# A two-layer hybrid trunk on one core: attention weights turned by transfers, heads joined on VectorE, squares read from SBUF, one lo stream tied behind both norms

## The chip, the cores and the metric

One core of one Trainium2 chip runs the whole program. The metric is the device time of one execution in microseconds, and the time of a kernel is the median of its runs. All matmuls, copies and transfers below are on this core's engines: TensorE (PE), VectorE (DVE), ScalarE (ACT), GpSimd (POOL) and the queue of SyncE (SP) that issues most of the transfers.

## The reference

A decoder trunk of two layers on 256 tokens of width 1024, in fp32. Each layer applies three sublayers, each followed by a LayerNorm of a residual:

```python
x <- LN(alpha*x + 0.5*SwiGLU_1(x))
x <- LN(alpha*x + Mixer(x))
x <- LN(alpha*x + 0.5*SwiGLU_2(x))
```

The mixer projects x to u, v, q, k, val and two gates. One branch is a gated position mixing of u and v. The other, which matters here, is differential attention: 8 heads, two softmax maps of head dimension 64 per head, and values of width 128.

```python
q, k = rope(q), rope(k)
p = softmax(where(causal, q @ k.T * scale, neg))       # two maps per head
a = p[:, :, 0] - lam * p[:, :, 1]
o = a @ val                                            # 128 wide per head
h_b = rmsnorm(o) * g * (1 - lam_init)
merge = sigmoid(gate_A)*(h_A W_A) + sigmoid(gate_B)*(h_B W_B)
```

## The kernel before, in words

**Products.** Every fp32 weight tile is split into a hi part (ACT copies it to fp32r, L174) and a lo part (DVE subtracts, L178, `wlo<-raw,whi`). A product then is hi x hi, lo x hi and hi x lo. `gemm_a2` does it for a 256-wide output: per half tile 8 matmuls of 512 columns against x's hi and lo side by side (L283), then, for the lo weights, 8 of 256 columns (L290). ACT copies one half of the bank to `r` (L291), DVE adds the other to give `z` (L293, or L295 with a scale). Pools are small: 4 raw tiles, 8 hi and 8 lo half tiles, 4 main PSUM banks and 4 side banks, each used in turn. A lo half tile is free again when the L290 that read its former content is done; a hi half tile when its L283 is.

**Order.** PE's instructions run as the program writes them (a manual schedule). A clock counts beats of PE work, some 2.8 us each; `beside(task, d)` lets a generator continue d beats later, and its `yield n` puts the rest off by n beats, so that work of other stages falls between the matmuls of a gemm. The other engines are ordered by a scheduler with priorities; `behind(ins)` ties an instruction behind another one on its engine.

**The attention part of the mixer.** After the values, four head pairs run. For each, `rope` makes q and then k: a `gemm_a2` of one tile, four small transfers on SP that swap the rotary halves (L809), POOL's multiplication of `swap` by the sines (L813), DVE's by the cosines (L812) and, tied behind the latest `z`, the addition `qk<-qk,swap` (L817). `attend` of a pair then runs beside the next pair's gemms:

- scores (L837), into two side banks for the second block of queries, and 0.6 beats later into two for the first; DVE masks and takes minima (L845), ACT exponentiates (L847);
- DVE forms the reciprocals and the weighted difference of the two maps (L863, L864, L856);
- 2.6 beats later PE transposes the difference in six 128x128 blocks (L871, L876) into two side banks, and ACT copies these to SBUF (L873, L878);
- 2.3 beats later PE multiplies with the values (L884, L886) into one side bank; ACT copies it to `on` (L889) and squares the bank in place for the sum of squares (L894);
- 2 beats later POOL makes the reciprocal root of four sums (L897, L256 to L264, called `rsqrt4`); 2 beats later ACT scales (L905), splits the 16-bit halves of each word into planes (L184), and one DMA transpose turns them (L189);
- after it has landed, ACT joins the planes (L195), and ACT and DVE write hi and lo of the head outputs (L915, L916).

So a pair takes seven side banks in turn: four for scores, two for transposes, one for the product. Gates follow the four pairs: `gemm_a2` and a tanh on ACT (L932), and their weights are split ahead, while the last pairs' attention still runs.

**The start of an FFN behind a norm.** `gemm_b2` starts with weights split early. The lo parts of its last stream are tied by `after[3]`. A norm's end for token half t is: statistics (L571, L578), a reciprocal root in eight tiny DVE instructions (L241 to L249), two 512-wide normalisations (L582), and PE's transposes of the result (L641). `norm.ends[t]` is the last L582 of half t; `norm.xlo[0, 1]` is a lo split of x that belongs to half 0, so it stands earlier.

Of the kernel before, what the change touches and what calls it, by code (L numbers as in the profile page):

```python
# [13 lines left out]
BF16 = mybir.dt.bfloat16  # L14
I32 = mybir.dt.int32
U16 = mybir.dt.uint16
# [4 lines left out]
P = 128  # L21
D = 1024
T = 256
# [35 lines left out]
def trunk(ctx, tc, x, xT, w13a, w13b, w2s, w2p, wb, wqk, wa, wbr, wo, gateb, sgug, sgub, sguwT, sgubias, lam, diffg,  # L59
# [129 lines left out]
        nc.sync.dma_start_transpose(out=tt.rearrange("p (c t) -> p c t", c=2 * n), in_=pk)  # L189
        return tt  # L190

    def join(dst, tt):

        with behind(emptied[0]):
            A.activation(dst.bitcast(U16).rearrange("p (k w) -> p k w", w=2), tt.rearrange("p (w k) -> p k w", w=2), AF.Copy)  # L195

    def ahead(srcs):

# [178 lines left out]
    def gemm_b2(srcs, xh, xl, done, norm=None):  # L377

        lent, after = [()] * 4, [(None, None)] * 4
        if norm:
            lent = [(0, 1), (0,), (), ()]
            after[1:3] = [(norm.ends[0], norm.ends[0])] * 2
        ps = [[bank() for _ in range(2)] for _ in range(NT)]
        got = [[None] * 4 for _ in range(2)]
        for t in range(NT):
            for c in range(2):
                if norm:
                    norm.ready(t, c)  # L390
                    after[3] = [norm.ends[1] if norm.pre else norm.xlo.get((0, 1))] * 2
                for m in range(2):
                    n = 2 * c + m
                    if t == 0 and n < 2 and norm and norm.pre:
                        if n == 0:
                            got[0][:2], got[1][:2] = rest_of(norm.pre, norm.ends[0])
                    elif t == 0:
                        got[m][2 * c : 2 * c + 2] = stream(srcs[m][:, c * CH : (c + 1) * CH], sub=512, lent=lent[n],
                                                           after=after[n])
                    for i in range(2 * c, 2 * c + 2):  # L400
                        rows_b(ps[t][m], t, 2 * i, got[m][i], xh, xl, KT)
            early[0] = None
            with behind(latest[0] if t == 0 else None):
                done(t, ps[t])
# [383 lines left out]
    def mixer(l, i, norm):  # L788
# [34 lines left out]
        def attend(hp, qT, kT):  # L823
# [38 lines left out]
            first = exps(0)  # L862
            V.reciprocal(out=rc, in_=sums[:, 4:])  # L863
            V.scalar_tensor_tensor(out=c4, in0=rc, scalar=neg_lam[l], in1=sums[:, :4], op0=ALU.mult, op1=ALU.mult)  # L864
            second, first = less(1, second), less(0, first)
            yield 2.6
            b = side_bank()
            for j in range(2):
                for c in range(2):
                    o = (j * 2 + c) * P  # L870
                    PE.transpose(b[:, o : o + P], second[:, o : o + P], ident)  # L871
            aT1 = slots("aT", 2)[0]
            A.activation(aT1, b, AF.Copy)  # L873
            b = side_bank()
            for j in range(2):
                PE.transpose(b[:, j * P : (j + 1) * P], first[:, j * P : (j + 1) * P], ident)  # L876
            aT0 = slots("aT", 2)[0][:, :T]
            A.activation(aT0, b[:, :T], AF.Copy)  # L878
            yield 2.3
            b = side_bank()  # L880
            for j in range(2):
                h = hp * 2 + j
# [5 lines left out]
            on = slots("on", 2)[0]  # L888
            A.activation(on, b, AF.Copy)  # L889
            ss, s2 = sm("ss", 4), sm("s2", 4)  # L890
            A.activation(s2, sums[:, :4], AF.Square, scale=(2 * HD * EPS) ** 0.5)
            for q in range(4):
                s = slice(q * P, (q + 1) * P)
                A.activation(b[:, s], b[:, s], AF.Square, accum_out=ss[:, q : q + 1])  # L894
            yield 2
            with behind(turned_by[0]):
                G.tensor_tensor(out=ss, in0=s2, in1=ss, op=ALU.add)  # L897
# [10 lines left out]
            tt = turning(pk, 4)  # L908
            yield LAND
            b = slots("turned", 2)[0]  # L910
            join(b, tt)
            dl = dgs[:, l : l + 1]
            for j in range(2):
                h, s = hb[hp * 2 + j], slice(j * T, (j + 1) * T)
# [194 lines left out]
```

## Time and the profile before

| | us |
|---|---|
| median of 3 runs | 1217.87 |
| lowest, highest run | 1216.63, 1217.92 |
| profiled execution, its own time | 1218.69 |
| its span in the trace | 1217.0 |
| granted TensorE clock, mean | 0.999 |

The span is what the trace covers; the 1.7 us between it and the execution's own time lie around it. In a timeline a row gives the start and the busy time in microseconds, the engine, the line, the operation, what is written from what, the shape and the count of instructions that the row groups; a bracket gives idle time before it on that engine and what ended it. In the waits, the three numbers are microseconds in total, times and the longest. In the windows, the columns are the window, its length and the busy time of PE, PEld, DVE, ACT and POOL with counts, then the granted clock, the share of the DMA engines and GB/s.

### The profile page before, as it was taken

Reading aid. Unit: us, or ns where it says so; the run is one execution under the profiler, and the core shown is the slowest. Engines: PE = TensorE matmul, PEld = TensorE weight load, DVE = VectorE, ACT = ScalarE, POOL = GpSimd, SP = SyncE. Lnnn points to the kernel's source line nnn. Section 1 sums busy time; section 2 is a strip of 40 time slices with the busy share of each in tenths; the row PEclk is TensorE's granted clock in tenths of the full one; section 3 lists DMA queues with packets and bytes.
Section 4 is the critical chain, followed back from the end, with each engine's and each line's share of the span. In section 5 each row is a group of like instructions: output and inputs, shape, how many; then the busy total and the mean of one; then the engine's idle time right before and its main releaser. Section 6 shows DMA issues by size and latency. Waiting matters only on the chain.

```text
span 1217.0 us, 16530 instructions
## 1 busy us (share of the span) xinstructions
PE 1205.4 (99%) x5961; PEld 1012.6 (83%) x5961; DVE 946.0 (78%) x1540; ACT 852.7 (70%) x1376; POOL 91.4 (8%) x184
## 2 busy tenths in 40 slices
PE   9999999999999999999999999999999999999998
PEld 8888888888888878888888888888888988788886
DVE  6658998875697876589985679988766878757797
ACT  6677677679865576776775776776898555667761
POOL 0100000223300000000000000003341000000000
PEclk9999999999999999999999999999999999999999
DMA  8985566655764748656677665766648456686551
GB/s 319 320 261 174 211 246 219 214 185 171 233 230 143 232 140 300 193 176 216 239 207 271 198 180 208 252 224 198 214 142 274 168 176 213 176 282 206 181 205 48
DMA packets 101346, 257.00 MB, mean 211 GB/s; under 512 B 66528, under 2 KB 67600, under 8 KB 74640
## 3 DMA queue, kind: packets, MB, share of 16 engines
q1 hardware_dynamic: 97296, 243.03, 59.8%
q0 software_dynamic: 3536, 12.13, 3.1%
q8 instruction: 46, 0.75, 0.2%
q10 hardware_dynamic: 432, 0.79, 0.2%
q14 instruction: 36, 0.29, 0.1%
HBM read 235.47 MB, written 1.05 MB: 194 GB/s over the span
## 4 chain that ended last, share of the span: by engine, by line
PE 91%; DVE 5%; ACT 2%; issue 1%; SPq 0%; DMA 0%; POOL 0%; DVEq 0%; ACTq 0%; POOLq 0%
PE bank L271 35%; PE sbank L271 24%; PE bank L283 16%; PE bank L290 8%; PE sbank L283 2%; PE bank L446 2%; PE sbank L290 1%; DVE wlo L178 1%; PE sbank L837 1%; PE sbank L969 1%; ACT pp L847 0%; ACT whi L174 0%; DVE nwa L248 0%; PE sbank L886 0%; DVE x L234 0%
## 5 line engine op out<-in xcount | busy, mean ns | idle before, releaser
L178 DVE TENSOR_TENSOR wlo<-raw,whi 128x1024 fp32r<-128x1024 f32 (+1 forms) x396 | 436.8, 1124 | 143.1 <-ACT whi L174 112.7
L174 ACT ACTIVATE whi<-raw 128x1024 fp32r<-128x1024 f32 (+1 forms) x396 | 372.9, 971 | 126.3 <-PE bank L283 44.9
L271 PE MATMUL bank<-whi,x 128*128 128x512 f32 x840 | 264.4, 391 | 0.0
L271 PEld LDWEIGHTS bank<-whi,x 128*128 128x128 f32 x840 | 158.6, 189 | 33.1
L271 PE MATMUL bank<-wlo,x 128*128 128x512 f32 x420 | 164.2, 391 | 0.0
L271 PE MATMUL sbank<-whi,x 128*128 128x512 f32 x512 | 158.9, 389 | 0.0
L283 PE MATMUL bank<-x,whi 128*128 128x512 f32 x640 | 156.0, 394 | 0.0
L283 PEld LDWEIGHTS bank<-x,whi 128*128 128x128 f32 x640 | 117.1, 188 | 26.4 <-issue 2.3
L271 PEld LDWEIGHTS sbank<-whi,x 128*128 128x128 f32 x512 | 96.1, 188 | 20.0
L353 ACT ACTIVATE shi<-raw 128x1024 fp32r<-128x1024 f32 (+1 forms) x80 | 73.4, 947 | 52.3 <-DVE raw L368 26.4
L271 PE MATMUL sbank<-wlo,x 128*128 128x512 f32 x256 | 99.6, 389 | 0.0
L355 DVE TENSOR_TENSOR slo<-raw,shi 128x1024 fp32r<-128x1024 f32 (+1 forms) x80 | 85.4, 1087 | 14.2 <-ACT shi L353 13.3
L271 PEld LDWEIGHTS bank<-wlo,x 128*128 128x128 f32 x420 | 79.2, 188 | 16.3
L290 PE MATMUL bank<-x,wlo 128*128 128x256 f32 x640 | 85.9, 285 | 0.0
L290 PEld LDWEIGHTS bank<-x,wlo 128*128 128x128 f32 x640 | 81.6, 191 | 2.2
L291 ACT ACTIVATE r<-bank 128x256 f32<-128x256 f32 x112 | 41.8, 377 | 24.5 <-PE bank L290 24.2
L271 PEld LDWEIGHTS sbank<-wlo,x 128*128 128x128 f32 x256 | 48.1, 188 | 9.9
L271 PE MATMUL sbank<-whi,hhi 128*128 128x512 f32 x144 | 56.3, 391 | 0.0
L271 PE MATMUL sbank<-whi,hlo 128*128 128x512 f32 x144 | 56.1, 389 | 0.0
L271 PE MATMUL sbank<-wlo,hhi 128*128 128x512 f32 x144 | 56.0, 389 | 0.0
L506 POOL DMA_DIRECT2D bc<-in_lng x6 | 3.2, 530 | 703.1 <-DVE bc L505 703.1
L710 ACT ACTIVATE planes<-silu 128x1024 uint16<-128x1024 uint16 x40 | 42.0, 1053 | 7.4 <-DVE silu L709 6.2
(249 smaller groups left out, 1996.8 us busy)
## 6 DMA issues: line engine op xcount, KB each, us to landing
raw<-in_w13b SPq DMA_DIRECT2D x76, 1024.0 KB, 5.4
raw<-in_w2p SPq DMA_DIRECT2D x24, 1024.0 KB, 4.9
raw<-in_wa SPq DMA_DIRECT2D x24, 1024.0 KB, 5.2
raw<-in_w2s SPq DMA_DIRECT2D x20, 1024.0 KB, 4.9
raw<-in_wb SPq DMA_DIRECT2D x16, 1024.0 KB, 5.3
raw<-in_wqk SPq DMA_DIRECT2D x16, 1024.0 KB, 4.9
raw<-in_wbr SPq DMA_DIRECT2D x16, 1024.0 KB, 4.8
raw<-in_w13a SPq DMA_DIRECT2D x8, 1024.0 KB, 4.8
```

The costliest lines, as they stand in the source:

```text
L174: copied = A.activation(h, r, AF.Copy)
L178: V.tensor_tensor(out=w, in0=r, in1=h.bitcast(F32), op=ALU.subtract)
L271: PE.matmul(ps, xx, w, start=start and n == 0, stop=stop and n == 2)
L283: PE.matmul(b[-1], hi[:, k * P : (k + 1) * P], xc(k), start=k == 0, stop=False)
L290: PE.matmul(b[n][:, :T], lo[:, k * P : (k + 1) * P], xc(k)[:, :T], start=False, stop=k == KT - 1)
L291: emptied[0] = A.activation(r[:, s], b[n][:, T:], AF.Copy, scale=scale).ins
L353: A.activation(h, r, AF.Copy)
L355: V.tensor_tensor(out=w, in0=r, in1=h.bitcast(F32), op=ALU.subtract)
L446: PE.matmul(ps[t][m], x[:, j, o + t * P : o + (t + 1) * P], y, start=k0 + j == 0 and o == 0 and y is hi, stop=k0 + j == KT - 1 and y is lo)
L710: A.activation(pk.rearrange("p (w k) -> p w k", w=2), s.bitcast(U16).rearrange("p (k w) -> p w k", w=2), AF.Copy)
L837: PE.matmul(banks[m][:, j * nk : (j + 1) * nk], rows(qT, m, j, t * P, P), rows(kT, m, j, 0, nk), start=True, stop=True)
L969: PE.matmul(b[:, j * T + t * P : j * T + (t + 1) * P], vg[t][:, g // 4, s], wsT[g // 4][:, s], start=True, stop=True)
```

## The change

Four edits:

1. The difference of the two maps is no longer transposed by PE. ACT splits it into planes, in a spare `pp` tile that held the other map; SP issues two DMA transposes; 3 beats later DVE joins the planes in two copies (1024 and 512 16-bit elements wide); 3.5 beats after that PE multiplies with the values. The PE transposes, their two side banks and ACT's two copies go. A pair takes five side banks instead of seven.
2. The squares read the SBUF copy `on` and write to a scratch tile, so the bank of the product is read only by the copy to `on`.
3. The join of the head outputs is on DVE, tied behind the latest `z`, instead of ACT.
4. The last lo stream at the start of an FFN is tied behind the norm's end of token half 1 in every case. Before, this held where the weights were split ahead (`norm.pre`), and otherwise (the second FFN of either layer, which follows the mixer) the tie was to `xlo[0, 1]`.

```diff
-    def join(dst, tt):
+    def joined(dst, tt):
 
-        with behind(emptied[0]):
-            A.activation(dst.bitcast(U16).rearrange("p (k w) -> p k w", w=2), tt.rearrange("p (w k) -> p k w", w=2), AF.Copy)
+        with behind(added[0]):
+            V.tensor_copy(dst.bitcast(U16).rearrange("p (k w) -> p k w", w=2), tt.rearrange("p (w k) -> p k w", w=2))
...
-                    after[3] = [norm.ends[1] if norm.pre else norm.xlo.get((0, 1))] * 2
+                    after[3] = [norm.ends[1]] * 2
...
+            free2, free1 = second[1], first[1]
             second, first = less(1, second), less(0, first)
-            yield 2.6
-            b = side_bank()
-            for j in range(2):
-                for c in range(2):
-                    o = (j * 2 + c) * P
-                    PE.transpose(b[:, o : o + P], second[:, o : o + P], ident)
-            aT1 = slots("aT", 2)[0]
-            A.activation(aT1, b, AF.Copy)
-            b = side_bank()
-            for j in range(2):
-                PE.transpose(b[:, j * P : (j + 1) * P], first[:, j * P : (j + 1) * P], ident)
-            aT0 = slots("aT", 2)[0][:, :T]
-            A.activation(aT0, b[:, :T], AF.Copy)
-            yield 2.3
+            half = slots("half", 2)[0]
+            tts = []
+            for (p, spare), dst in (((second, free2), slots("tt", 2)[0]), ((first, free1), half[:, :T])):
+                pk = spare.bitcast(U16)
+                planes(pk, p)
+                tts.append(turning(pk, pk.shape[1] // (2 * P), dst))
+            yield 3
+            aT1, aT0 = slots("aT", 2)[0], half[:, T:]
+            for dst, tt in zip((aT1, aT0), tts):
+                joined(dst, tt)
+            yield 3.5
...
+            junk = s512("junk").bitcast(BF16)
...
-                A.activation(b[:, s], b[:, s], AF.Square, accum_out=ss[:, q : q + 1])
+                A.activation(junk[:, s], on[:, s], AF.Square, accum_out=ss[:, q : q + 1])
...
-            join(b, tt)
+            joined(b, tt)
```

Up to L864 the two kernels have the same line numbers; behind it the new ones are one or two lower for the same code: L889, L905 and L932 of before are L887, L904 and L931 of after.

On DVE, in layer 0, where the scores of the second head pair have been masked and the third pair's `rope` ends (`qk_2336` before and `qk_2333` after are the same rotated k; L856 is the difference of the maps), the rows before are

```order
L845 ISA mx_2315 128x1
L863 RECIPROCAL rc_2318<-sums_2316 128x4
L178 TENSOR_TENSOR wlo_2767<-raw_2764,whi_2766 128x1024
L864 SCALAR_TENSOR_TENSOR c_2317<-rc_2318,neg_lam_818,sums_2316 128x4
L295 SCALAR_TENSOR_TENSOR z_2394<-bank_2353,r_2393 128x256
L856 SCALAR_TENSOR_TENSOR pp_2325<-pp_2330,c_2317,pp_2325 128x256 x2
L856 SCALAR_TENSOR_TENSOR pp_2368<-pp_2373,c_2317,pp_2368 128x128 x2
L817 TENSOR_TENSOR qk_2336<-qk_2336,swap_2335 128x512
L295 SCALAR_TENSOR_TENSOR z_2394<-bank_2384,r_2393 128x256
L178 TENSOR_TENSOR wlo_2771<-raw_2764,whi_2770 128x1024
L812 TENSOR_TENSOR qk_2433<-z_2394,cos_t 128x512
L178 TENSOR_TENSOR wlo_2865<-raw_2862,whi_2864 128x1024
```

and after

```order
L863 RECIPROCAL rc_2315<-sums_2313 128x4
L178 TENSOR_TENSOR wlo_2741<-raw_2734,whi_2740 128x1024
L864 SCALAR_TENSOR_TENSOR c_2314<-rc_2315,neg_lam_818,sums_2313 128x4
L856 SCALAR_TENSOR_TENSOR pp_2322<-pp_2327,c_2314,pp_2322 128x256 x2
L856 SCALAR_TENSOR_TENSOR pp_2365<-pp_2370,c_2314,pp_2365 128x128 x2
L178 TENSOR_TENSOR wlo_2840<-raw_2837,whi_2839 128x1024
L178 TENSOR_TENSOR wlo_2844<-raw_2837,whi_2843 128x1024
L295 SCALAR_TENSOR_TENSOR z_2397<-bank_2350,r_2396 128x256
L817 TENSOR_TENSOR qk_2333<-qk_2333,swap_2332 128x512
L295 SCALAR_TENSOR_TENSOR z_2397<-bank_2387,r_2396 128x256
L812 TENSOR_TENSOR qk_2420<-z_2397,cos_t 128x512
```

Two lo splits and a `z` now stand between L856 and L817, where a `z` ahead of L856 and nothing behind it stood. At the same place one pair earlier there are three splits and a `z` between them now, and nothing before; there the first two splits belong to an earlier tile than the third.

On ACT, in layer 0, around the copy `on` of the second head pair (`on_2636` before, `on_2677` after; `both` is the scaled output of the first pair, `gate` a gate's tanh), the rows before are

```order
L174 ACTIVATE whi_2965<-raw_2959 128x1024
L291 ACTIVATE r_2609<-bank_2568 128x256
L905 ACTIVATE both_2621<-on_2412,nwy_2510 128x128 x4
L184 ACTIVATE both_2621<-both_2621 128x1024
L291 ACTIVATE r_2609<-bank_2599 128x256
L889 ACTIVATE on_2636<-sbank_2629 128x512
L894 ACTIVATE sbank_2629,ss_2638<-sbank_2629 128x128
L174 ACTIVATE whi_3037<-raw_3035 128x1024
```

and after

```order
L184 ACTIVATE pp_2513<-pp_2508 128x1024
L184 ACTIVATE pp_2560<-pp_2555 128x512
L904 ACTIVATE both_2662<-on_2462,nwy_2604 128x128 x4
L174 ACTIVATE whi_3008<-raw_3002 128x1024
L931 ACTIVATE gate_2526<-gz_2611,gbh 128x256 x2
L184 ACTIVATE both_2662<-both_2662 128x1024
L291 ACTIVATE r_2687<-bank_2644 128x256
L291 ACTIVATE r_2687<-bank_2653 128x256
L174 ACTIVATE whi_3081<-raw_3079 128x1024
L887 ACTIVATE on_2677<-sbank_2670 128x512
```

Between the four scalings and `on` there now stand two hi copies and two gate activations as well. `nwy_2604` is POOL's reciprocal root of the first pair; on POOL its instructions stand behind the sine multiplication of the fourth pair's k (`swap_2518`) after the change, and before that multiplication in the kernel before.

On DVE, at the start of the second FFN of layer 0 (`xtok_144` is the residual of token half 1, `yi` to `nwy` its reciprocal root), the rows before are

```order
L244 TENSOR_SCALAR yi_4365<-ve_4364 128x1
L178 TENSOR_TENSOR wlo_4502<-raw_4499,whi_4501 128x512
L248 TENSOR_SCALAR nwa_4368<-yi_4365,ve_4364 128x1
L178 TENSOR_TENSOR wlo_4502<-raw_4499,whi_4501 128x512
L249 TENSOR_SCALAR nwy_4369<-nwa_4368,yi_4365 128x1
L178 TENSOR_TENSOR wlo_4508<-raw_4499,whi_4507 128x512
L248 TENSOR_SCALAR nwa_4372<-nwy_4369,ve_4364 128x1
L178 TENSOR_TENSOR wlo_4508<-raw_4499,whi_4507 128x512
L249 TENSOR_SCALAR nwy_4373<-nwa_4372,nwy_4369 128x1
L248 TENSOR_SCALAR nwa_4376<-nwy_4373,ve_4364 128x1
L249 TENSOR_SCALAR nwy_4377<-nwa_4376,nwy_4373 128x1
L582 TENSOR_SCALAR xtok_144<-xtok_144,mv_4362,nwy_4377 128x512 x2
```

and after

```order
L244 TENSOR_SCALAR yi_4357<-ve_4356 128x1
L248 TENSOR_SCALAR nwa_4360<-yi_4357,ve_4356 128x1
L249 TENSOR_SCALAR nwy_4361<-nwa_4360,yi_4357 128x1
L248 TENSOR_SCALAR nwa_4364<-nwy_4361,ve_4356 128x1
L249 TENSOR_SCALAR nwy_4365<-nwa_4364,nwy_4361 128x1
L248 TENSOR_SCALAR nwa_4368<-nwy_4365,ve_4356 128x1
L249 TENSOR_SCALAR nwy_4369<-nwa_4368,nwy_4365 128x1
L582 TENSOR_SCALAR xtok_144<-xtok_144,mv_4354,nwy_4369 128x512 x2
L178 TENSOR_TENSOR wlo_4494<-raw_4491,whi_4493 128x512 x2
L178 TENSOR_TENSOR wlo_4500<-raw_4491,whi_4499 128x512 x2
```

The four lo splits of the last stream have moved from between the steps of the reciprocal root to behind the normalisation.

## The prediction

> **What bounds the kernel now.** I read the page first: busy time and the chain of work that ended last.
>
> ```profile
> PE 1205.4 (99%) x5961; PEld 1012.6 (83%) x5961; DVE 946.0 (78%) x1540; ACT 852.7 (70%) x1376; POOL 91.4 (8%) x184
> ```
>
> ```profile
> PE 91%; DVE 5%; ACT 2%; issue 1%; SPq 0%; DMA 0%; POOL 0%; DVEq 0%; ACTq 0%; POOLq 0%
> ```
>
> TensorE is busy for 1205.4 of 1217.0 us. The other engines matter only where a matmul waits for them, so the time can change in two ways: PE gets less work, or PE's waits (some 11.6 us in all) change. An engine with 22% idle time can still delay PE if one instruction stands behind the wrong neighbour. The largest wait that this change touches, as total, number and longest:
>
> ```profile
> PE sbank L641 <- DVE xtok L582: 4.7, 2, 2.4
> ```
>
> So I went through PE's timeline of the mixer in layer 0, then DVE, POOL and ACT at the same places, against the new order of instructions. Layer 1 has the same order, so each sum is doubled.
>
> **What it takes away.** First the six PE transposes per head pair. Two stretches of a rotary gemm, from its second hi half to the next score matmuls, without transposes and with:
>
> ```profile
> 222.23 3.82 PE L283 MATMUL bank<-x,whi 128*128 128x512 f32 x16
> 225.88 2.07 PE L290 MATMUL bank<-x,wlo 128*128 128x256 f32 x16
> 227.88 1.14 PE L837 MATMUL sbank<-qk,qk 64*128 64x256 f32 x8
> ```
>
> ```profile
> 235.52 3.82 PE L283 MATMUL bank<-x,whi 128*128 128x512 f32 x16
> 239.18 0.60 PE L871 MATMUL sbank<-ident,pp 128*128 128x128 f32 x4
> ...
> 241.84 1.13 PE L837 MATMUL sbank<-qk,qk 64*128 64x256 f32 x8
> 244.97 0.71 PE L837 MATMUL sbank<-qk,qk 64*128 64x128 f32 x8
> ```
>
> Without: 227.88 − 222.23 = 5.65. With: 241.84 − 235.52 = 6.32. A pair's transposes cost 0.67 us; eight pairs, **−5.4 us**. The Trainium skill speaks against this edit: "VectorE: DVE Perf Modes", section The three transpose paths, prices a 128x128 bf16 transpose at 390 ns on TensorE and 1309 ns by the DMA crossbar. By 390 ns the 48 transposes would be an estimated 18.7 us, which the trace does not bear out.
>
> In their place come two plane copies on ACT, two DMA transposes and two copies on DVE per pair. The nearest transfer and the nearest copy:
>
> ```profile
> tt<-both SPq DMA_TRANSPOSE x8, 2.8
> ```
>
> ```profile
> L195 ACT ACTIVATE turned<-tt x8: 1168/1177/1187, 287.3 to 923.5; 128x1024 uint16<-128x1024 uint16 x8
> ```
>
> A transfer lands 2.8 us after its issue, and the weights are joined 3 beats (some 8 us) after the planes; the attention-value matmuls come 3.5 beats later still. Two transfers in turn (5.6 us) fit, so I cost the path at nothing; if the cover went, one late transfer would cost PE up to 2.8. SP's queue takes 16 more issues between weight loads that run several tiles ahead: nothing. The copies' length on DVE is not in the trace; between 0.6 of ACT's 1.17 for the large one with half of that for the small one (0.9–1.0) and ACT's own speed (1.7). I keep both ends and take 1.2. ACT loses two copies and the join, gains two plane copies: near even. The join of heads on DVE is off PE's path.
>
> Second, the squares read the SBUF copy, so a side bank is free again once it has been copied. The waits hold one for the old squares:
>
> ```profile
> PEld sbank L837 <- ACT sbank L894: 0.5, 1, 0.5
> ```
>
> It goes, **−0.5**.
>
> Third, the norm. Two ends of a norm on DVE, the first for t=0 and the second for t=1, from the rsqrt's start to the normalisation:
>
> ```profile
> 417.07 0.15 DVE L244 TENSOR_SCALAR yi<-ve 128x1 int32<-128x1 int32 x1
> ...
> 431.18 0.15 DVE L244 TENSOR_SCALAR yi<-ve 128x1 int32<-128x1 int32 x1
> ```
>
> ```profile
> 418.94 1.00 DVE L582 TENSOR_SCALAR xtok<-xtok,mv,nwy 128x512 f32<-128x512 f32 x2
> 434.94 1.00 DVE L582 TENSOR_SCALAR xtok<-xtok,mv,nwy 128x512 f32<-128x512 f32 x2
> ```
>
> t=0 takes 418.94 − 417.07 = 1.87; t=1, with lo splits between its small steps, 434.94 − 431.18 = 3.76. In the new order four of the splits stand behind L582, so 1.89 goes from the wait, twice: **−3.8**. The splits come back after L582, needed by PE only some matmuls after the transposes: nothing.
>
> The wait that shrinks to about 0.5 us also has a follower. After one of the two, the granted clock falls:
>
> ```profile
> 436.00:440.00 4.00, 4.00 (x13) 3.29 (x14) 0.69 (x1) 2.71 (x6) 0.00 (x0) 0.59 0.86 287
> 1038.00:1042.00 4.00, 3.55 (x18) 3.00 (x19) 1.05 (x2) 3.17 (x6) 0.00 (x0) 1.00 1.37 293
> ```
>
> 0.59 in the first (4 us x 0.41 = 1.64 us of matmul time lost), 1.00 in the second, after waits that sum to 4.7 with a longest of 2.4. That drop should go: **−1.6**. The Trainium skill, "TensorE: Matmul & The Clock Gate", section What's actually happening, has the clock halved after an idle window of about 3.4 us; this drop came after a shorter wait, so the trace does not follow the figure. By the figure, among the waits below only the third would bring a drop, which is what the sum has too. Gains together: 5.4 + 0.5 + 3.8 + 1.6 = **−11.3**.
>
> **What it adds.** Taking steps out moved others. Three places of the mixer.
>
> *Places 1 and 2: rotary addition (L817) behind the lo splits.* In the old order L817 stood right behind L856. Now, for the second pair, three splits stand between, of which the last waits until PE's L290 has freed its lo buffer; for the third pair there are two, and both wait so. The score matmuls (L837) need L817 as soon as L290 ends. DVE's rows beside the L290 of 225.88:
>
> ```profile
> 227.10 1.23 DVE L178 TENSOR_TENSOR wlo<-raw,whi 128x1024 fp32r<-128x1024 f32 x1 [0.90 <-PE bank L290]
> 228.25 0.75 DVE L293 TENSOR_TENSOR z<-bank,r 128x256 f32<-128x256 f32 x2
> ```
>
> ```profile
> 252.47 0.69 DVE L817 TENSOR_TENSOR qk<-qk,swap 128x512 f32<-128x512 f32 x1
> ```
>
> The first split that needs a buffer of this L290 starts 227.10 − 225.88 = 1.22 after it began, takes 228.25 − 227.10 = 1.15; one z is 0.37 (half of 0.75); L817 0.69. Together 3.43 after L290's start, which itself lasts 227.88 − 225.88 = 2.00. PE waits **+1.43** at place 1, and one more split, 1.15, makes it **+2.58** at place 2. None of these waits stands in the trace of before.
>
> *Place 3: the score matmuls of the fourth pair behind the `on` copy.* Their second block needs the side bank of the second pair's attention-value product, freed by ACT's copy to `on`. That copy now stands behind L905 for the first pair (four scalings), a gate pair, the planes, two r copies and a hi copy; the scalings need POOL's rsqrt, which now stands behind one more swap multiplication. The steps begin at the third pair's L837, whose start I call S; the rows are those of the pair before it (241.84):
>
> ```profile
> 242.19 0.75 DVE L293 TENSOR_TENSOR z<-bank,r 128x256 f32<-128x256 f32 x2
> ```
>
> ```profile
> 244.41 0.41 DVE L845 CUSTOM_DVE_ANT_0 pp<-sbank,mask 128x256 f32<-128x256 f32 x1
> ...
> 245.79 0.68 DVE L812 TENSOR_TENSOR qk<-z,cos_t 128x512 f32<-128x512 f32 x1
> ```
>
> ```profile
> 247.06 1.30 POOL L813 TENSOR_TENSOR swap<-swap,sin_t 128x512 f32<-128x512 f32 x1 [3.65 <-DMA swap<-z]
> ```
>
> ```profile
> 259.86 0.20 POOL L897 TENSOR_TENSOR ss<-s,ss 128x4 f32<-128x4 f32 x1
> ...
> 265.80 1.29 POOL L813 TENSOR_TENSOR swap<-swap,sin_t 128x512 f32<-128x512 f32 x1
> ```
>
> DVE: L837 itself 1.13 (row of 241.84), four L845 245.79 − 244.41 = 1.38, z 0.75, the copies 1.2: 4.46. From z's end (242.94) to POOL's multiplication, through the swap DMAs, 4.12; that 1.30; the rsqrt chain 265.80 − 259.86 = 5.94. So far S + 15.8. Then ACT:
>
> ```profile
> 266.85 1.27 ACT L905 ACTIVATE both<-on,nwy 128x128 f32<-128x128 f32 x4
> 268.15 1.06 ACT L184 ACTIVATE both<-both 128x1024 uint16<-128x1024 uint16 x1
> 269.11 0.36 ACT L291 ACTIVATE r<-bank 128x256 f32<-128x256 f32 x1
> 269.38 0.59 ACT L889 ACTIVATE on<-sbank 128x512 f32<-128x512 f32 x1
> ```
>
> ```profile
> 276.47 0.91 ACT L932 ACTIVATE gate<-gz,gbh 128x256 f32<-128x256 f32 x2 [1.08 <-DVE gz L293]
> ```
>
> ```profile
> 292.72 2.97 ACT L174 ACTIVATE whi<-raw 128x1024 fp32r<-128x1024 f32 x3
> ```
>
> By starts: L905 1.30, L184 0.96, two r 0.54, `on` 0.59; gates 0.91; two hi copies 1.98. Together 6.28, so the bank is free at S + 22.1 (21.8 to 22.5). PE is there earlier. Its next pair's scores follow 257.12 − 241.84 = 15.28 later, less a pair's transposes, and their second block 244.97 − 241.84 = 3.13 after that:
>
> ```profile
> 257.12 1.13 PE L837 MATMUL sbank<-qk,qk 64*128 64x256 f32 x8
> ```
>
> 15.28 − 0.67 + 3.13 = 17.74. PE waits **+4.3** (4.0 to 4.8). Its floor: were POOL in time, the last hi copy (0.99) and `on` (0.59) still follow each other behind PE's release, **+1.6**.
>
> Per layer 1.43 + 2.58 + 4.3 = 8.3, for two 16.6. A 4.3 us wait is longer than the one after which the clock fell: a drop behind the longest wait of each layer, 2 x 1.64 = 3.3.
>
> **Sum.** −11.3 + 16.6 + 3.3 = +8.6. The profiled execution took 1218.69 (span 1217.0), so by it 1227.3; the median of the three runs is 1217.87, 0.8 lower, so **1226.5**, given as 1226. A change of 0.2%, 2.4 us, is about what a measurement can tell from none.
>
> **The rivals.**
>
> *The third wait at its floor, no clock drop.* POOL may receive its swap early enough. Then −11.3 + 2 x (1.43 + 2.58 + 1.6) = −0.1: 1217.8. For it: POOL is 8% busy. Against: POOL's multiplication waited 3.65 for its swap at 247.06, so it is the transfer, not POOL, that sets the time. 0.17.
>
> *A clock drop behind every new wait.* −11.3 + 16.6 + 6 x 1.64 = +15.1: 1233. For: the drop at 436 came after a wait of at most 2.4, near place 2's 2.58. Against: its twin showed none, and 1.43 is far shorter. 0.15.
>
> *Faster: the lo splits do not hold L817 up.* If those that wait for L290 have their buffers earlier than by the row at 227.10, L817 is done in time and places 1 and 2 cost nothing; it decides whether L817 ends within 2.00 of L290's start. Then −11.3 + 2 x 4.3 = −2.7, with no drop: 1215.2. Less than that if the third wait is short as well. For: DVE has 22% idle. Against: this split too stood in a wait for L290:
>
> ```profile
> 256.34 1.23 DVE L178 TENSOR_TENSOR wlo<-raw,whi 128x1024 fp32r<-128x1024 f32 x1 [1.11 <-PE bank L290]
> ```
>
> 0.20. By the skill's 390 ns, removed transposes would bring 13.3 more than by the rows (an estimate, 1213); since the stretch of 6.32 holds six of them and all else, I give that 0.01, counted in here.
>
> **How the numbers follow.** The forecast has 0.45; with it the drops behind every wait and 0.03 for a stall that I missed are slower, 0.63; same 0.17; faster 0.20. The range, 1215 to 1232, holds the forecast with its own spread (1223 to 1229, from the copies' length and one clock drop more or less), the floor case, most of the faster case, and a third of the case with every drop: 0.45 + 0.17 + 0.13 + 0.05.
>
> **What would show it.** PE's busy time falls by some 5. Waits of L837 (the old number) for DVE's `qk`, twice per layer, 1.4 and 2.6, and for ACT's `on` once per layer, 4.3; L641's wait for L582 near 0.5; granted clock 1.0 behind L641 and below 1.0 behind the longest wait. I am wrong if those waits of L837 are absent, or if L641's wait stays at 2.4.

## The result, and the profile after

The changed kernel takes 1236.03 us (median of 4 runs, 1235.14 to 1237.29) against 1217.89 (4 runs, 1216.63 to 1219.05): a ratio of 1.0149, 95% interval 1.0132 to 1.0165. It is slower by 18 us where 8 were forecast; 1236 lies above the range that ended at 1232. The profiled execution took 1235.17, with a span of 1233.5, 16.5 more than the span of before; the sums below are made on these two spans.

The page of the changed kernel, busy time and the chain that ended last:

```profile
PE 1204.6 (98%) x5913; PEld 1010.8 (82%) x5913; DVE 964.3 (78%) x1564; ACT 850.3 (69%) x1368; POOL 94.6 (8%) x184
...
PE 82%; DVE 8%; ACT 3%; POOL 3%; issue 2%; DMA 2%; SPq 0%; DVEq 0%; POOLq 0%; ACTq 0%
```

TensorE has 48 transposes less and is busy for almost as long (1204.6 against 1205.4): some of its matmuls must have run slower. And its share of the chain fell from 91% to 82%. The chain now runs through DVE, ACT, POOL and transfers. The waits name the places (total, times, longest):

```profile
PE sbank L837 <- ACT on L887: 10.0, 2, 5.4
...
PE sbank L837 <- DVE qk L817: 7.7, 4, 2.5
...
PE sbank L968 <- DVE vg L950: 3.2, 2, 1.7
```

None of the three is among the waits of before. The first two are those of the forecast, in the places that it named; the third was not forecast. In PE's timeline of layer 0 the brackets are the idle time ahead of a row:

```profile
242.07 1.13 PE L837 MATMUL sbank<-qk,qk 64*128 64x256 f32 x8 [1.35 <-DVE qk L817]
...
259.26 1.13 PE L837 MATMUL sbank<-qk,qk 64*128 64x256 f32 x8 [2.49 <-DVE qk L817]
260.32 3.55 PE L283 MATMUL bank<-x,whi 128*128 128x512 f32 x8
...
278.53 0.48 PE L837 MATMUL sbank<-qk,qk 64*128 64x128 f32 x2
283.65 1.22 PE L837 MATMUL sbank<-qk,qk 64*128 64x128 f32 x6 [4.63 <-ACT on L887]
284.80 3.54 PE L283 MATMUL bank<-x,whi 128*128 128x512 f32 x8
```

Eight matmuls of L283 take 2.14 where the clock is full; behind the two longer waits they take 3.5. The windows (last columns: granted clock, share of the DMA engines, GB/s) show the clock there, and behind the same wait in layer 1:

```profile
260.00:264.00 4.00, 4.00 (x14) 2.48 (x12) 3.34 (x13) 2.71 (x11) 0.00 (x0) 0.58 0.92 301
284.00:288.00 4.00, 4.00 (x14) 3.10 (x13) 1.84 (x14) 4.00 (x20) 2.01 (x10) 0.51 0.76 246
892.00:896.00 4.00, 2.57 (x9) 2.08 (x10) 3.62 (x20) 4.00 (x16) 0.73 (x4) 0.51 0.88 276
```

DVE at place 1 and, second, at place 2. Each has two splits in a row, one z and the addition, which ends 0.1 before PE goes on:

```profile
238.53 2.55 DVE L178 TENSOR_TENSOR wlo<-raw,whi 128x1024 fp32r<-128x1024 f32 x2 [0.98 <-ACT whi L174]
241.00 0.42 DVE L295 SCALAR_TENSOR_TENSOR z<-bank,r 128x256 f32<-128x256 f32 x1
241.34 0.68 DVE L817 TENSOR_TENSOR qk<-qk,swap 128x512 f32<-128x512 f32 x1
...
255.91 2.36 DVE L178 TENSOR_TENSOR wlo<-raw,whi 128x1024 fp32r<-128x1024 f32 x2 [1.21 <-ACT pp L184]
258.19 0.42 DVE L295 SCALAR_TENSOR_TENSOR z<-bank,r 128x256 f32<-128x256 f32 x1
258.52 0.68 DVE L817 TENSOR_TENSOR qk<-qk,swap 128x512 f32<-128x512 f32 x1
```

The bracket of 255.91 names ACT's plane copy, but the splits need nothing of it. The start lies 1.29 behind that of L290 (254.62), and 1.30 in layer 1 (865.21 to 866.51), as 1.22 and 1.30 in the kernel before (225.88 to 227.10, 255.04 to 256.34): the freed lo buffer fits it. At place 1 the first of the two splits started before L290 (238.65) and had waited for ACT's hi copy. It ended at about 239.8 (238.53 + 1.23), as the second one's buffer came free (1.22 to 1.30 behind 238.65, by the rows of before). So at place 1 the late hi copy alone would have cost about as much.

And place 3, first POOL (the multiplications of the fourth pair's q and k, then the first pair's root), then ACT (that pair's scalings, and the copy that PE waits for):

```profile
266.82 1.30 POOL L813 TENSOR_TENSOR swap<-swap,sin_t 128x512 f32<-128x512 f32 x1 [14.78 <-DMA swap<-z]
268.34 2.03 POOL L813 TENSOR_TENSOR swap<-swap,sin_t 128x512 f32<-128x512 f32 x1 [0.21 <-DMA swap<-z]
270.33 0.64 POOL L896 TENSOR_TENSOR ss<-s,ss 128x4 f32<-128x4 f32 x1
```

```profile
277.66 1.28 ACT L904 ACTIVATE both<-on,nwy 128x128 f32<-128x128 f32 x4 [3.07 <-POOL nwy L264]
...
283.01 0.58 ACT L887 ACTIVATE on<-sbank 128x512 f32<-128x512 f32 x1
```

From 259.26, the S of the prediction, to the end of `on` it took 24.3 us (22.1 forecast). At the norm the wait is what was forecast:

```profile
444.49 0.66 PE L641 MATMUL sbank<-ident,xtok 128*128 128x128 f32 x4 [0.47 <-DVE xtok L582]
```

The third wait, of the spatial matmuls L968, comes from the last pair's output. DVE, which now joins it, waits for its transfer, and ACT stands behind DVE; a hi copy and the gelu of v (L938, `vg`) come next in its row:

```profile
333.29 0.69 DVE L195 COPY turned<-tt 128x1024 uint16<-128x1024 uint16 x1 [2.91 <-DMA tt<-both]
```

```profile
334.01 0.91 ACT L914 ACTIVATE hb<-turned,dgs 128x256 fp32r<-128x256 f32 x2 [3.66 <-DVE turned L195]
```

```profile
359.07 0.94 PE L968 MATMUL sbank<-wsT,vg 128*128 128x128 f32 x6 [1.50 <-DVE vg L950]
```

The transfer was issued 4.35 after the start of v's gemm (324.99 against 320.64), where before it was 1.72 (313.70 against 311.98); it landed 12.65 after that start, before 8.91. The first gelu starts 16.55 after the start of v's gemm (337.19), before 14.10 (326.08), and the L950 that the waiting matmuls need 37.63 after it (358.27), before 35.19 (347.17): the delay of 2.4 goes down the row unchanged. L968 comes to wait for what is left of it.

Stage by stage, from the distances between the same instructions in the two traces:

| term, both layers | forecast | measured |
|---|---|---|
| transposes | −5.4 | −5.4 |
| bank of the scores | −0.5 | −0.8 |
| norm | −3.8 | −3.8 |
| clock drop behind the norm | −1.6 | −1.6 |
| place 1 | +2.9 | +2.8 |
| place 2 | +5.2 | +5.2 |
| place 3 | +8.6 | +10.0 |
| clock drops | +3.3 | +7.0 |
| spatial matmuls (L968) | not forecast | +3.7 |
| start of the program | | −0.5 |
| sum | +8.6 | +16.6 |

The 0.5 at the start stands ahead of anything that the change touches. The transposes' value is that of the mended kernel below, put in here so that places 1 and 2 can be read from the distances. The clock drops are 1.5 behind place 2 in layer 0 only, and 2.5 and 3.0 behind place 3, worked out as what is left of the distance from the fourth pair's scores to the next gemm when the wait, the transposes and, in layer 0, the 0.8 of the bank are taken off.

### The profile page after: what moved, and what is told of

Same layout as the page of the kernel before. It is cut to its first block, busy times and chain, and to the rows that moved or that the text cites. A ratio compares the mean times of both kernels' runs of the same rounds, so it can differ in the third digit from the quotient of the medians.

```text
span 1233.5 us, 16517 instructions
## 1 busy us (share of the span) xinstructions
PE 1204.6 (98%) x5913; PEld 1010.8 (82%) x5913; DVE 964.3 (78%) x1564; ACT 850.3 (69%) x1368; POOL 94.6 (8%) x184
## 4 chain that ended last, share of the span: by engine, by line
PE 82%; DVE 8%; ACT 3%; POOL 3%; issue 2%; DMA 2%; SPq 0%; DVEq 0%; POOLq 0%; ACTq 0%
PE bank L271 32%; PE sbank L271 23%; PE bank L283 13%; PE bank L290 6%; PE sbank L283 2%; DVE wlo L178 2%; PE bank L446 2%; PE sbank L290 1%; PE sbank L837 1%; ACT whi L174 1%; DMA tt<-both 1%; DVE nwa L248 1%; DMA swap<-z 1%; PE sbank L968 1%; DVE nwy L249 1%
## 5 line engine op out<-in xcount | busy, mean ns | idle before, releaser
L283 PE MATMUL bank<-x,whi 128*128 128x512 f32 x640 | 160.5, 402 | 0.0
L283 PEld LDWEIGHTS bank<-x,whi 128*128 128x128 f32 x640 | 120.1, 193 | 27.5 <-issue 1.7
L290 PE MATMUL bank<-x,wlo 128*128 128x256 f32 x640 | 84.3, 285 | 0.0
L290 PEld LDWEIGHTS bank<-x,wlo 128*128 128x128 f32 x640 | 81.7, 192 | 2.4
```

Of the source, the lines that this page charges most:

```text
L283: PE.matmul(b[-1], hi[:, k * P : (k + 1) * P], xc(k), start=k == 0, stop=False)
L290: PE.matmul(b[n][:, :T], lo[:, k * P : (k + 1) * P], xc(k)[:, :T], start=False, stop=k == KT - 1)
```

## The experiments

The theory: the time is lost in waits behind instructions that the new order has put in front, and in clock drops behind these waits; the transfers, plane copies and joins themselves cost TensorE nothing. The rival: they make the attention path longer as such, and a better order would only shift the wait. All ratios below are to the kernel before in the same series, with 95% intervals.

**The addition untied.** In `rest()`:

```diff
-                with behind(None if last else added[0]):
+                with behind(None):
```

> The changed kernel, with the rotary addition (L817) no longer tied behind the latest z, so that it stands right behind the difference of the maps again, ahead of the lo splits. Theory (the time is lost in waits behind instructions that the new order has put in front): the four waits of L837 for the rotated qk, 7.7 us in the changed kernel, fall below 0.5, and the clock drop behind one of them (1.5) goes; the waits for the copy `on` (10.0 in 2) stay. 1236 - 7.7 - 1.5 = 1227, between 1225 and 1230. Rival (the transfers and the copies on VectorE make it late by their own length, so a place in the row ahead changes little): half of the 7.7 or more stays, 1232 or more.

1232.19 us, ratio 1.0118 (1.0102 to 1.0135): slower than the theory's range. Its waits, total, times and longest:

```profile
PE sbank L837 <- ACT on L887: 9.1, 2, 5.5
...
PE sbank L837 <- DVE qk L817: 3.6, 2, 1.9
```

The timeline shows no wait for qk at places 1 and 2. The 3.6 are two new ones: the fourth pair's scores, which TensorE now reaches earlier, wait for their own addition, and a clock drop follows that of layer 0. So the mechanism at places 1 and 2 is shown, and so is that more than half of the gain (9 expected, 4 found) is given back one pair later.

**The root earlier.** In `attend`:

```diff
+            tie = turned_by[0]
             yield 2
-            with behind(turned_by[0]):
+            with behind(tie):
```

> The changed kernel, with the reciprocal root of a pair tied behind the swap multiplication that was the latest when its squares were issued, and not two beats later; so the first pair's root stands ahead of the fourth pair's multiplication on GpSimd, as in the kernel before. Theory: the two waits of L837 for `on` (10.0 us, longest 5.4) fall to at most 1.6 each, and the clock drops behind them (2.5 and 3.0) go; the waits for qk stay at 7.7. 1236 - 6.8 - 5.5 = 1224, between 1221 and 1229. Rival (the copy `on` is late because ScalarE has more to do, with the planes of the weights): the waits stay above 3 each and the drops stay, 1231 or more.

1226.25 us, ratio 1.0067 (1.0056 to 1.0079), within the theory's range. The waits for `on` fall to some 0.65 each, and the waits of L968 (L969 in this kernel), which the expectation left out, to one of 0.66. Two waits for qk came in at the fourth pair, layer 0's being:

```profile
276.47 1.14 PE L837 MATMUL sbank<-qk,qk 64*128 64x256 f32 x8 [2.32 <-DVE qk L817]
```

**Both edits together.**

> Both edits together: the addition untied and the root tied earlier. Theory: only what the change takes away is left, and the wait of the spatial matmuls (L968, 3.2 us in 2, 3.7 by the distance of the stages), which these edits do not touch: 1236.0 - 7.7 - 10.0 - 7.0 (all clock drops) = 1211, between 1209 and 1215, faster than before. Rival (the transfers and copies cost PE time as such, or another wait takes the place): 1218 or more.

1226.28 us, ratio 1.0067 (1.0056 to 1.0079): the theory's 1211 is wrong here, and another wait has taken the place, as its rival said. It is one of 7.0 and one of 6.8, for the fourth pair's addition. POOL's rows in layer 0:

```profile
264.45 1.61 POOL L813 TENSOR_TENSOR swap<-swap,sin_t 128x512 f32<-128x512 f32 x1 [11.55 <-DMA swap<-z]
266.03 0.19 POOL L897 TENSOR_TENSOR ss<-s,ss 128x4 f32<-128x4 f32 x1
...
272.05 1.27 POOL L813 TENSOR_TENSOR swap<-swap,sin_t 128x512 f32<-128x512 f32 x1
```

POOL is 7% busy in this kernel, but here it has the swap of q, six microseconds of root and the swap of k in a row, and TensorE needs either the root (through ACT's scalings and `on`) or the multiplication next. In the kernel before the same row of three began at 258.61, 13.8 ahead of the fourth pair's scores (272.40); here it begins at 264.45, only 6.2 before TensorE comes for them (277.71 − 7.04).

**The other three edits alone.** The kernel before with the squares from SBUF, the heads' join on DVE and the norm's tie.

```diff
-                    after[3] = [norm.ends[1] if norm.pre else norm.xlo.get((0, 1))] * 2
+                    after[3] = [norm.ends[1]] * 2
...
-                A.activation(b[:, s], b[:, s], AF.Square, accum_out=ss[:, q : q + 1])
+                A.activation(junk[:, s], on[:, s], AF.Square, accum_out=ss[:, q : q + 1])
...
-        with behind(emptied[0]):
-            A.activation(dst.bitcast(U16).rearrange("p (k w) -> p k w", w=2), tt.rearrange("p (w k) -> p k w", w=2), AF.Copy)
+        with behind(added[0]):
+            V.tensor_copy(dst.bitcast(U16).rearrange("p (k w) -> p k w", w=2), tt.rearrange("p (w k) -> p k w", w=2))
```

> The kernel before with edits 2, 3 and 4 alone: squares from SBUF, the heads' join on VectorE, the last lo stream behind both norms; the weights are still transposed by TensorE. Theory: the places 1 to 3 come with the turned weights and their longer distances alone, so none of their waits is there; what is left is the norm's 3.8, the clock drop's 1.6 and a bank wait of 0.8: 1217.9 - 6.2 = 1212, between 1210 and 1214. First rival (the join on VectorE is what holds ScalarE and so the spatial matmuls up): 3.7 more, 1215.5. Second rival (the waits come from the side banks that the squares free earlier, which moves the rest): 1222 or more.

1211.87 us, ratio 0.9950 (0.9939 to 0.9961): the theory's number. None of the waits of L837 or L968 is there, so the join on DVE is not what holds the spatial matmuls up by itself.

**The norm's tie alone** (the first of the diffs above).

> The kernel before with the fourth edit alone, the last lo stream behind both norms. Theory: the waits of L641 shrink by 1.9 in each layer and the clock drop behind the first goes (1.6): 1218 - 5.4 = 1212.6, between 1211 and 1214.5. Rival (the 0.8 of the bank and other parts carry the gain of the fourth experiment, and a norm's wait comes back later as a wait for the four late splits): 1215 or more.

1212.70 us, ratio 0.9961 (0.9949 to 0.9974). The wait of L641 is 0.45 in layer 0 and 0.44 in layer 1, and the clock stays full behind both. So most of the gain is this one line. By the medians it is 4.1, by the two profiled spans 6.1: in that series the runs of the kernel before lie between 1215.98 and 1220.15, those of this kernel between 1212.48 and 1212.97.

**The turned weights alone.** The kernel before with the first edit; the join of the weights on DVE, that of the heads on ACT.

> The kernel before with the first edit alone: weights by transfers, longer distances; the squares still read the bank, the heads' join is on ScalarE, the lo stream tied as before. Theory (the first edit brings all three places; the other three edits are worth 6.2 by the fourth experiment): 1236.0 + 6.2 = 1242, or more, since the fourth pair's bank is freed only by the squares, which stand behind `on`: between 1240 and 1250, the waits for qk at 7.7 again. Rival (the squares' edit, which frees banks earlier, is what moves the order at place 3): the long waits of L837 for a bank are not there, 1233 or less.

1248.28 us, ratio 1.0255 (1.0238 to 1.0272), in the theory's range: the first edit alone loses 30 us, and the other three give back more beside it (12) than on their own (6). The waits for qk are 1.35 and 2.49 in each layer again; that of L968 is 5.1 in 2. The heads' join is on ACT here, so L968's waits do not need the join on DVE. The norm's 4.7 is back, with a clock drop in both layers. The fourth pair's second block waits 4.9 in 2, less than in the changed kernel where the expectation had more, and not for `on`:

```profile
281.60 1.22 PE L842 MATMUL sbank<-qk,qk 64*128 64x128 f32 x6 [2.60 <-DVE mx L850]
```

L842 and L850 are L837 and L845 there. `on` is written only at 284.20, behind the end of this wait; TensorE waited for DVE's masking of the fourth pair's first block. Ahead of that, DVE had a lo split that waited 3.80 for ACT's hi copy, and ACT had the scalings ahead of the copy, which waited 3.15 for POOL's root. The late root holds TensorE up in this kernel too, but by another way than the bank of the product.

**The short distances.**

```diff
-            yield 3
+            yield 2.6
...
-            yield 3.5
+            yield 2.3
```

> The changed kernel with the two distances of the kernel before, 2.6 and 2.3 beats in place of 3 and 3.5, so that the attention-value product comes 1.6 beats earlier; the weights still go by transfers. In the order of instructions one lo split instead of two now stands ahead of the third pair's addition, and the first pair's root stands ahead of the fourth pair's multiplication; the three splits of place 1 stay. Theory (the longer distances push the root and the last pair's outputs into the next stage's way; the transfers are not to blame): the wait for qk at place 1 stays at 1.35, that at place 2 falls to some 1.3, the waits for `on` fall below 1.6, their drops go, and the wait of L968 goes: 1236 - 2.4 - 6.8 - 7.0 - 3.7 = 1216, between 1212 and 1222. Rival (distance does not matter, or the transfers do not land in the shorter time and PE waits for them): 1229 or more.

1221.52 us, ratio 1.0025 (1.0012 to 1.0039): near the end of the theory's range. The waits at place 2 and of L968 are gone, and one of 0.9 for `on` is left; place 1 stays at 1.35. What the theory had not is waits of L283 for a bank that a gate's addition on DVE empties (3.2 in 4) and, again, the fourth pair's addition, 1.72 and 2.47:

```profile
273.09 1.14 PE L837 MATMUL sbank<-qk,qk 64*128 64x256 f32 x8 [1.72 <-DVE qk L817]
```

No attention-value matmul waits for its weights, so the transfers land in 2.6 + 2.3 beats as well. The longer distances of the change are worth some 15 us of its loss.

**The short distances and the addition untied.**

> The fifth experiment's kernel (short distances), with the rotary addition untied as in the first. Theory (behind places 1 and 2 the next limit is GpSimd, whose root stands ahead of the fourth pair's multiplication): the two waits of 1.35 at place 1 go, and TensorE comes to the fourth pair's wait by as much earlier, so that grows from 1.7 and 2.5 to some 3 and 3.8: 1221.5 - 0 to 1, between 1219 and 1223 with a clock drop more or less. Rival (each wait is worth itself): 2.7 less, 1218 or below.

1219.24 us, ratio 1.0018 (1.0009 to 1.0027). The waits at place 1 are gone, those at the fourth pair have grown to 3.01 and 3.14, as the theory had it. Here the twin waits differ in the clock: a drop at 274 behind the first, none behind the second.

**The splits tied later.** Three kernels tie the lo splits of the rotary and gate gemms behind the z of the gemm before the last: alone, with the earlier root, and with the short distances.

```diff
-            got += stream(src)
+            got += stream(src, after=(ended[0], ended[0]) if tied else (None, None))
...
+                ended[:] = ended[1], a.ins
```

> The changed kernel with the lo splits of the mixer's gemms tied behind the z of the gemm before the last, so that no split stands ahead of the z and the additions of places 1 and 2. Theory (splits that run ahead and wait for a buffer hold up what stands behind them): the waits for qk go (7.7), and the clock drop behind place 2 (1.5); the swaps are issued earlier, so GpSimd's root comes earlier and the waits for `on` get shorter by some 2 each: 1236 - 7.7 - 1.5 - 4 = 1223, between 1218 and 1228. Rival (a later split makes TensorE wait for its lo weights, which takes the gain back): a wait of L290 for wlo L178 in the waits, 1231 or more.

> The same with the root tied earlier too, as in the second experiment. Theory: the swap of the fourth pair's q is early now, so the root and behind it the multiplication for k are done before TensorE needs either; the fourth pair's addition, which waited 7.0 in each layer in the third experiment, waits no more; what is left is the spatial matmuls' wait at most: 1217.9 - 11.6 + 3.7 = 1210, between 1206 and 1214. Rival (GpSimd's time, root and multiplication in a row, is the limit whatever stands ahead on VectorE): the fourth pair's wait stays at 5 or more per layer, 1218 or more.

> Splits tied as in the two before, and the short distances of the fifth experiment, with the root where it falls. Theory: no wait of places 1 to 3 and none of L968 is left, the weights land in time: 1217.9 - 11.6 = 1206, between 1204 and 1210. Rival (at the short distance the transfers land too late, or the late splits make L290 wait): a wait of the attention-value matmuls for the joined weights, or of L290 for wlo, 1212 or more.

1238.76, 1230.61 and 1226.09 us (ratios 1.0165, 1.0101 and 1.0062; intervals 1.0145 to 1.0185, 1.0082 to 1.0120, 1.0041 to 1.0084): the theory's numbers are missed three times, by 16 to 21 us. The waits for qk do go in all three. In the first the waits for `on` stay (9.4 in 3), and U's gemm waits for a bank that DVE empties late (5.1 in 2, and 5.3 in the second kernel). The rival's wait, of L290 for its lo weights, is 1.1 to 1.4 per layer in the first two and the largest in the third (L290 is L292 there):

```profile
PE bank L292 <- DVE wlo L178: 7.3, 4, 2.1
```

A split that comes later is needed before it is done. Tied this way the splits are no cure; the additions have to come forward instead.

**The order mended at all three places.** On the changed kernel: short distances, the addition untied, the root later so that it stands behind both multiplications, and ACT's scalings behind the next pair's `on`.

```diff
-            A.activation(on, b, AF.Copy)
+            kept[0] = A.activation(on, b, AF.Copy).ins
...
-            yield 2
+            yield 2 if hp == HEADS // 2 - 1 else 3.2
             with behind(turned_by[0]):
...
-            yield 2
+            yield 2 if hp == HEADS // 2 - 1 else 2.6
...
-                with behind(emptied[0]):
+                with behind(kept[0]):
```

> The changed kernel with its order mended at all three places: short distances to the product, the addition untied, the root issued 3.2 beats behind the squares so that it stands behind the fourth pair's multiplication, and the scalings of ScalarE tied behind the next pair's copy `on` (2.6 beats behind the root; the last pair 2 and 2 as before). Theory: no wait of L837 is left and the 5.4 of the transposes is kept: 1218 - 11.6 = 1206.5, between 1204 and 1210. Rival (the transfers, the plane copies and the joins cost what the transposes did, in other waits): 1212 or more, no better than edits 2 to 4 alone.

1209.34 us, ratio 0.9934 (0.9917 to 0.9951), in the theory's range: faster than the kernel before by 0.7% (1216.75 in its series) and than the changed one by 27 us. The page:

```profile
PE 1197.7 (99%) x5913; PEld 1006.2 (83%) x5913; DVE 963.1 (80%) x1564; ACT 849.1 (70%) x1368; POOL 87.9 (7%) x184
```

TensorE's busy time is 7.7 below that of before: the 5.4 of the transposes, the 1.6 of the clock drop, and 0.7 over. Two small waits are left that the kernel before did not have:

```profile
PE bank L283 <- DVE z L295: 1.4, 2, 1.0
PE sbank L837 <- DVE qk L817: 1.1, 2, 0.7
```

The row of the fourth pair's scores shows 0.39 of idle time ahead in layer 0, and 0.68 in layer 1. The distance of the first two score blocks is 13.29 (227.68 to 240.97) against 13.96: the 0.67 of the prediction. With the same transfers, plane copies and joins as the changed kernel, TensorE has the gain of the transposes, and 2.5 of it goes into the two small waits. The span is 9.1 below that of before, which is the first four rows of the table, 11.6, less these 2.5. In the same series the norm's tie alone took 1212.70, so this kernel is 3.4 faster than that. Edits 2 and 3 may hold some 0.8 of this (1212.70 against 1211.87 for edits 2 to 4, in another series), so the turned weights bring an estimated 2.6 of their 5.4. The rival, that the path eats the whole gain whatever the order, does not hold for this order.

## Why the prediction was wrong

**What held.** The bound (TensorE, and the waits of TensorE), the gains and the three places. Their mechanisms held too, but for the late hi copy at place 1, which the forecast did not have. Place 1 was forecast at 1.43 and place 2 at 2.58 in each layer; measured by distances, 1.42 and 2.58 (the brackets show 1.35 and 2.49; the rest, under 0.1, passes between the end on DVE and the start on PE). The norm's −3.8 and the −1.6 behind it came as forecast, and the norm's tie alone brings them. The transposes' 0.67 per pair is confirmed by the mended kernel. By the Trainium skill, "VectorE: DVE Perf Modes", section The three transpose paths, which has 390 ns for a 128x128 bf16 transpose on TensorE, an estimated 18.7 us would have gone; the traces, with fp32 transposes, show 5.4. The change as it stands did lose time by moving them to transfers, and the mended order, with the same transfers, shows that the order did this, not the transfers.

**One of the two steps that failed most, 3.7 us: "a drop behind the longest wait of each layer, 2 x 1.64 = 3.3".** The mechanism was right, the size was not: 7.0. The price came from a drop behind a wait of 2.4, which had 1.6 of slow matmuls behind it. Behind the waits of about 5 us 2.5 and 3.0 were lost, and a third drop (1.5) came behind place 2 in layer 0, which the prediction kept for a rival. The length of the wait does not set the price either. Behind a wait of 6.83 (third experiment, layer 1) and one of 2.49 (turned weights alone, layer 1) the windows show, in this order (the clock is the third number from the right):

```profile
884.00:892.00 8.00, 8.00 (x39) 5.97 (x40) 6.00 (x24) 7.40 (x31) 3.15 (x15) 0.80 0.89 289
875.00:883.00 8.00, 7.83 (x29) 5.48 (x30) 5.37 (x18) 4.45 (x15) 1.10 (x1) 0.59 0.60 182
```

The longer wait lost 1.6 (8 us x 0.20), the shorter 3.3 (8 us x 0.41). A drop seen once was no price for the next. The prediction's rival, "a clock drop behind every new wait", was nearest with 1233, but not right either: three of the six waits had one.

**The other, also 3.7, was missing: who waits for the last pair's outputs.** "The join of heads on DVE is off PE's path" is false in the changed kernel: ACT's rows behind it, the gelu of v among them, came late enough for L968 to wait 1.5 and 1.7, and 3.7 by the distance of the stages. The root is place 3, not the join: in the kernel with the first addition untied, where the waits for `on` stayed, L968 waits 2.9; in the two with the earlier root, the two with short distances and the mended one, where they went or fell to at most 1.3, it does not wait but for one 0.66, with the join on DVE in all of them. With the turned weights alone and the join on ACT it waits 5.1. That ties the two waits together over these kernels; no experiment delayed the last pair's outputs alone. The three kernels with splits tied later have waits of their own there and are not counted.

**The step that was mis-sized: place 3, 4.3 forecast, 4.63 and 5.35 measured.** The rows of a calmer place were used. The multiplication on POOL took 2.03 instead of 1.30 and the root 7.3 (270.33 to 277.66) instead of 5.94, while DVE was at work beside it; ACT's rows took 5.9 instead of 6.28 (277.66 to 283.59). What slowed the root is not shown; the next one, with DVE idle beside most of it, took 4.3 (285.24 to 289.50). That 4.3 and 4.63 lie so close is partly luck: in layer 0 the bank came free 2.2 later than forecast (24.3 behind S), but PE came to it 2.0 later as well (279.02, S + 19.8, where 17.7 were forecast), 1.5 of it by the clock drop behind place 2 and 0.5 because the block's first two matmuls did not need that bank. In layer 1, where place 2 had no drop, the wait was 5.35. The copies on DVE took 0.94 by starts (245.37 to 246.31), near the low end; the forecast had taken 1.2.

**Rivals.** The third wait at its floor was not seen. The faster case named the point that decides, L817 done within 2.00 of L290's start; at place 1 it only began 2.69 behind that start (238.65 to 241.34). The range ended at 1232 because most of the case with every drop was left out, and because a stall that the text did not name had a chance but no price.

## What to carry to other kernels

When a change takes work from the bound engine, read what the new order puts ahead of each instruction for which that engine waits, on every queue behind it, and follow the latest output of the stage to its last reader. Price a wait with the clock drop that may follow, as a range: here 1.5 to 3.3 us, or nothing. Mending one place shows the next one, so a gain is to be counted only when the whole chain has been moved.

## What the runs showed of the hardware

**The granted clock can fall behind a wait of 1.65 us, and need not behind one of 3.14.** Waits at the same place of the two layers, in one execution each: 2.36 with a drop and 2.34 without (before); 2.49 with and 2.49 without (changed kernel); 2.49 without and 2.49 with (root earlier); 1.85 with and 1.80 without (addition untied; a gap of 0.43 follows the 1.85); 1.68 without and 1.65 with (splits tied later, earlier root); 3.01 with and 3.14 without (short distances and untied). Every wait of TensorE of 3.6 or more in the mixers had one (3.64, 3.85, 4.06, 4.40, 4.63, 5.35, 5.50, 6.83, 7.04). Behind the 1.65, the shortest wait with a drop here, the eight matmuls that take 2.14 at full clock take 3.63 (L840 and L285 are L837 and L283):

```profile
887.16 0.71 PE L840 MATMUL sbank<-qk,qk 64*128 64x128 f32 x6 [1.65 <-ACT on L890]
887.80 3.63 PE L285 MATMUL bank<-x,whi 128*128 128x512 f32 x8
```

The Trainium skill, "TensorE: Matmul & The Clock Gate", section What's actually happening, has the clock fall after an idle window of about 3.4 us, and the windows run freely: the start of a kernel does not reset them. A free-running window would explain that one twin is hit and the other is not; but a whole idle window does not fit into 1.65 us, so the traces disagree with that part.

**POOL and DVE can slow each other down.** In the changed kernel POOL's multiplication of 268.34 took 2.03 and DVE's addition beside it 1.78, where each takes 1.30 and 0.68 by itself:

```profile
269.13 1.78 DVE L817 TENSOR_TENSOR qk<-qk,swap 128x512 f32<-128x512 f32 x1
```

It is not always both: POOL's multiplication of 246.45 took 1.31, and DVE's multiplication (L812) beside it 1.32 instead of 0.68. What they share was not tried.

**A 16-bit copy of 1024 elements per partition** takes 0.69 on DVE (L195), against 1.17 for the same join on ACT.
